# Second norm's squares on ScalarE and adds on VectorE, gate/up operands written between products, last transposes a group later

## Chip, cores and metric

The kernel runs on one core of a Trainium2 chip. The metric is the time of one execution in device microseconds, and the time of a kernel is the median of its runs. In the text PE is TensorE, PEld its weight loads, DVE VectorE, ACT ScalarE, POOL GpSimd and SP SyncE; ACT, DVE, POOL and SP also issue transfers. L1208 is line 1208 of the kernel before; lines of the kernel after are named as such.

## The reference

One decoder layer on x of 512 tokens by 1024 features, all float32. The part around the change is the second half:

```python
mix = jnp.concatenate([y_ml, y_ssd, y_ret], axis=-1)
x = x + mix @ w_out
h = rmsnorm(x, norm_ffn)                      # x * rsqrt(mean(x*x) + 1e-6) * g
gate, up = jnp.split(h @ w_gate_up, 2, axis=-1)
return x + (jax.nn.silu(gate) * up) @ w_down  # then the final rmsnorm
```

Ahead of it stand the first rmsnorm, one wide input projection, and three groups of mixer heads (mLSTM, Mamba-2, retention), which the change does not touch.

## The kernel before

Each float32 matmul is done as three on pairs: an operand is split into `hi` (rounded to float32r) and `lo` (the rest), and a product is hi·hi + hi·lo + lo·hi. Weights come in chunks of 128x1024; `split` (L211, L212) makes a chunk's `hi` by a cast on ACT and its `lo` by a subtraction on DVE. There are four buffers of each, and PE frees one when it has used a chunk, so the splits run some three chunks ahead of PE.

**Output projection.** `products_f` (L427 to L429) multiplies the mixer's result by w_out. `ev_out` evacuates each of eight row blocks x2[k] (L1160, DVE, from PSUM plus the residual), scales it by the norm's weight into y2 (L1164, ACT) and stores x2d (L1165). For odd blocks of the first four it also makes the operands "11" and "S3" with `split_a`: a cast on ACT (L1147) and a subtraction on DVE (L1148).

**Gate and up.** The columns go in blocks p of widths 5x512 and 256. Each block is seven products in the manner of Strassen, "11", "S3", "S1", "S2", "12", "S4", "22" in this order (`product`; L1207 takes `hi` of both, L1208 the weights' `lo`, L1209 the operand's `lo`). Each reads two chunks of weights and one operand of y2, or a sum of blocks of y2 made by `combine` (L1153). Some weight chunks are themselves sums: on `big` buffers they are added by DVE (L952), or by an accumulating load that POOL issues (L194), which waits for the earlier load into the same buffer. `more_loads` issues two such quarters.

**Second norm.** `Norm.feed` squares the x2 blocks in place, the odd ones on POOL (L328), the even ones on ACT (L330), and adds them in a tree on POOL (L334). `finish` sums over the partitions by four matmuls with ones (L340), copies the result (L342, ACT), and takes the power -1/2 on POOL (L306, L286). The result `r2` scales the gate inside the Silu (L1270, ACT), so the products need not wait for it.

**Transposes and down projection.** `turn` makes closures that transpose 128x128 tiles of silu(gate)·up (L1218); `turn_one` runs one between later products. The last of them run in the down projection. That one goes over chunks n and row groups c, each with two banks; for n = 0 the residual is transposed into the banks first (L1314), then L1317 to L1319 multiply. Operands are split by `split_t` (ACT, and POOL at L1296).

**Order.** A scheduler sets the order on each engine from its own estimates, on the basis of the order of the code, except for what is wrapped in `pin`, which keeps its place. An engine runs its instructions in that order; one that waits holds up all behind it.

Of the kernel before, what the change touches and what calls it, by code (L numbers as in the profile page):

```python
# [11 lines left out]
AF = mybir.ActivationFunctionType  # L12
ALU = mybir.AluOpType
# [3 lines left out]
P = 128  # L17
# [102 lines left out]
def trunk(tc, x, xt, wcat, vecs, rows, consts, posn, gfin, out):  # L120
# [6 lines left out]
    with contextlib.ExitStack() as es:  # L127
# [190 lines left out]
        class Norm:  # L318
# [836 lines left out]
        for last in (False, True):  # L1155
            for gr in range(2):

                def ev_out(t, ps):
                    d = x2[4 * gr + t]
                    dve.tensor_tensor(out=d, in0=ps, in1=d, op=ALU.add)  # L1160
                    if last:
# [3 lines left out]
                        sp.dma_start(out=x2d[k], in_=d)  # L1165
                        if t % 2 and gr == 0:
# [13 lines left out]
        s1 = [combine(dve, halves(i, 1), halves(2 + i, 1), ALU.subtract) for i in range(2)]  # L1180
        for i in range(2):
            split_a("S1", i, s1[i])
        s2 = [combine(dve, s1[i], halves(i, 0), ALU.subtract) for i in range(2)]
        for i in range(2):
            split_a("S2", i, s2[i])
        for i in range(2):
            split_a("12", i, halves(2 + i, 0))
        s4 = [combine(pool, halves(2 + i, 0), s2[i], ALU.add) for i in range(2)]
        for i in range(2):
            split_a("22", i, halves(2 + i, 1))  # L1190
        for i in range(2):
            split_a("S4", i, s4[i])
        for k in range(KD):
            n2.feed(x2[k], k % 2 == 1, adds=pool, own=False)
        more_loads()
# [38 lines left out]
        for p, w in enumerate(GU_W):  # L1234
# [4 lines left out]
            for c in range(2):  # L1239
                act.copy(out=s1[c], in_=ba[c][:, 0:w])  # L1240
            bb = [bank() for _ in range(2)]
            product(bb, "S3", w, True)
            e = [slot(w=w) for _ in range(2)]
# [8 lines left out]
            product(bq, "S1", w, True)  # L1252
            turn_one()
            product(bb, "S2", w, False)
            if p == 0:
                n2.finish(r2)
# [10 lines left out]
            product(ba, "12", w, False)  # L1267
            g1 = [slot(w=w) for _ in range(2)]
# [32 lines left out]
        for n, kc in enumerate(DOWN_ORDER):  # L1301
            w2 = [chunk(), chunk()]
            split_t(n + 2)
            for c in range(NC):
                if n == 0 and c == 2:
                    while tail:
                        turn_one()
                    banks += [mbank() for _ in range(4)]
                for hf in range(2):
                    whi, wlo = w2[hf]  # L1310
                    o_ = banks[2 * c + hf]
                    if n == 0:
                        for k in range(4):
                            mm(o_[:, k * P:(k + 1) * P], lhsT=x2[4 * hf + k][:, c * P:(c + 1) * P], rhs=ident, start=k == 0, stop=False, is_transpose=True)  # L1314
                    for k in range(2):
                        ah, al = (t[:, c * P:(c + 1) * P] for t in asp[2 * kc + k])
                        mm(o_, lhsT=ah, rhs=whi[:, k, :], start=False, stop=False)  # L1317
                        mm(o_, lhsT=ah, rhs=wlo[:, k, :], start=False, stop=False)  # L1318
                        mm(o_, lhsT=al, rhs=whi[:, k, :], start=False, stop=n == NK2 - 1 and k == 1)  # L1319
                if n == NK2 - 1:  # L1320
                    ss, rf = small(2, "ssf", bufs=4), small(1, "rf", bufs=4)
                    t = [slot() for _ in range(2)]
                    for hf in range(2):
                        o_ = banks[2 * c + hf]
                        act.activation(out=t[hf], in_=o_, func=AF.Square, accum_out=ss[:, hf:hf + 1])
                    pool.tensor_scalar(out=ss[:, 0:1], in0=ss[:, 0:1], scalar1=1.0 / D, scalar2=EPS, op0=ALU.mult, op1=ALU.add)
                    dve.scalar_tensor_tensor(out=rf, in0=ss[:, 1:2], scalar=1.0 / D, in1=ss[:, 0:1], op0=ALU.mult, op1=ALU.add)
                    rsq(rf)
                    for hf in range(2):
                        y = slot()  # L1330
                        dve.tensor_tensor(out=y, in0=banks[2 * c + hf], in1=gf[hf], op=ALU.mult)
                        if hf == 0:
                            act.activation(out=y, in_=y, func=AF.Copy, scale=rf)
                        else:
                            dve.tensor_scalar(out=y, in0=y, scalar1=rf, scalar2=None, op0=ALU.mult)
                        (act if hf else sp).dma_start(out=out[c, :, 512 * hf:512 * hf + 512], in_=y)
# [70 lines left out]
```

## Time and profile before

| | |
|---|---|
| time, median of 3 runs | 846.32 us (844.91 to 847.32) |
| profiled execution | 845.48 us, span 843.7 us |
| mean granted clock of TensorE | 0.996 |
| busy: PE, PEld | 826.8 us (98%), 710.7 us (84%) |
| busy: DVE, ACT, POOL | 536.7 us (64%), 382.8 us (45%), 256.2 us (30%) |
| transfers | 110.72 MB, mean 131 GB/s |

PE is busy nearly all of the span. What can be gained without taking matmuls away are the places at which it waits, and those at which it runs below its full clock. The wide table of groups counts for little here; the list of waits, the timelines of single engines and the table of stretches tell what stands at such a place.

### The profile page before, as it was taken

What the parts mean: (1) busy time and instruction counts of PE and PEld (TensorE: products, weight loads), DVE (VectorE), ACT (ScalarE), POOL (GpSimd) and SP (SyncE); (2) the same over time, 40 slices, a digit from 0 to 9 for tenths busy, and PEclk for the clock granted to TensorE, in tenths of its full rate; (3) what the DMA queues carried; (4) which work ended last, traced back from release to release, by engine and by line L of the source; (5) the groups of instructions that cost most, each with busy time, mean ns of one, the idle gap of its engine ahead of it and who ended that gap; (6) DMA issues with size and microseconds to landing.
All of it is one profiled execution on the core that took longest, in us unless ns stands there. A gap on an engine that the chain in (4) does not pass through costs nothing.

```text
span 843.7 us, 11298 instructions
## 1 busy us (share of the span) xinstructions
PE 826.8 (98%) x4238; PEld 710.7 (84%) x4238; DVE 536.7 (64%) x760; ACT 382.8 (45%) x655; POOL 256.2 (30%) x261
## 2 busy tenths in 40 slices
PE   9999999999999899999999989999999999999997
PEld 8989889898988788888888868888888889788885
DVE  6648667594739878466633799887878778332223
ACT  6344535464534354335312474646455557511113
POOL 3234524242013966531600573000010103840001
PEclk9999999999999999999999999999999999999999
DMA  7423242332323323224823469686675559330002
GB/s 254 157 65 120 83 142 83 94 113 88 101 83 98 119 76 125 75 75 151 274 101 113 125 191 245 198 252 175 183 190 139 107 147 385 124 100 0 1 1 99
DMA packets 38262, 110.72 MB, mean 131 GB/s; under 512 B 4392, under 2 KB 4776, under 8 KB 38208
## 3 DMA queue, kind: packets, MB, share of 16 engines
q1 hardware_dynamic: 33744, 96.93, 34.2%
q0 software_dynamic: 3456, 11.54, 7.8%
q10 hardware_dynamic: 1008, 1.54, 0.5%
q8 instruction: 33, 0.54, 0.3%
q14 instruction: 21, 0.17, 0.1%
HBM read 104.70 MB, written 5.29 MB: 130 GB/s over the span
## 4 chain that ended last, share of the span: by engine, by line
PE 62%; DVE 5%; POOL 2%; issue 1%; DMA 1%; ACT 1%; POOLq 0%; SPq 0%; ACTq 0%; DVEq 0%
PE b L1207 6%; PE b L1209 6%; PE b L1208 6%; PE b L428 4%; PE b L427 4%; PE b L429 4%; PE b L409 3%; PE b L411 3%; PE b L410 3%; PE m L1208 3%; PE m L1209 2%; PE m L1207 2%; PE m L1319 2%; PE m L1318 2%; PE m L1317 2%; PE b L1317 2%
## 5 line engine op out<-in xcount | busy, mean ns | idle before, releaser
L212 DVE TENSOR_TENSOR lo<-raw,hi 128x1024 fp32r<-128x1024 f32 (+3 forms) x97 | 118.2, 1222 | 116.1 <-ACT hi L211 115.7
L211 ACT CAST hi<-raw 128x1024 fp32r<-128x1024 f32 (+3 forms) x106 | 103.2, 977 | 149.3 <-PE b L428 77.4
L212 DVE TENSOR_TENSOR lo<-big,hi 128x1024 fp32r<-128x1024 f32 (+1 forms) x79 | 97.3, 1234 | 88.3 <-ACT hi L211 86.0
L211 ACT CAST hi<-big 128x1024 fp32r<-128x1024 f32 (+1 forms) x79 | 78.1, 991 | 125.7 <-PE m L1319 57.3
L427 PE MATMUL b<-s,hi 128*128 128x512 f32 x304 | 120.1, 396 | 0.8 <-ACT s L677 0.8
L428 PE MATMUL b<-s,hi 128*128 128x512 f32 x304 | 119.0, 392 | 0.0
L429 PE MATMUL b<-s,lo 128*128 128x512 f32 x304 | 118.5, 391 | 0.0
L410 PE MATMUL b<-lo,s 128*128 128x384 f32 (+2 forms) x320 | 115.2, 360 | 0.8 <-DVE lo L212 0.8
L409 PE MATMUL b<-hi,s 128*128 128x384 f32 (+2 forms) x320 | 114.2, 366 | 0.0
L411 PE MATMUL b<-hi,s 128*128 128x384 f32 (+2 forms) x320 | 113.6, 361 | 0.0
L1208 PE MATMUL b<-lo,s 128*128 128x512 f32 (+1 forms) x240 | 89.7, 374 | 0.0
L1209 PE MATMUL b<-hi,s 128*128 128x512 f32 (+1 forms) x240 | 89.3, 372 | 0.0
L1207 PE MATMUL b<-hi,s 128*128 128x512 f32 (+1 forms) x240 | 88.6, 378 | 0.0
L427 PEld LDWEIGHTS b<-s,hi 128*128 128x128 f32 x304 | 57.1, 188 | 12.1 <-ACT s L677 1.1
L429 PEld LDWEIGHTS b<-s,lo 128*128 128x128 f32 x304 | 57.1, 188 | 11.6
L428 PEld LDWEIGHTS b<-s,hi 128*128 128x128 f32 x304 | 57.2, 188 | 11.0
L410 PEld LDWEIGHTS b<-lo,s 128*128 128x128 f32 x320 | 60.2, 188 | 6.0 <-DVE lo L212 1.2
L409 PEld LDWEIGHTS b<-hi,s 128*128 128x128 f32 x320 | 60.0, 188 | 5.1 <-ACT hi L211 0.3
L411 PEld LDWEIGHTS b<-hi,s 128*128 128x128 f32 x320 | 59.9, 188 | 4.9
L658 DVE SCALAR_TENSOR_TENSOR s<-s,vec,s 128x511 f32<-128x511 f32 (+2 forms) x66 | 58.4, 928 | 0.2 <-ACT s L655 0.2
L194 POOL DMA_DIRECT2D big<-in_wcat x19 | 16.8, 884 | 136.4 <-DMA big<-in_wcat 105.3
L1208 PEld LDWEIGHTS b<-lo,s 128*128 128x128 f32 x240 | 45.3, 189 | 8.0 <-DVE lo L212 0.3
(294 smaller groups left out, 1560.0 us busy)
## 6 DMA issues: line engine op xcount, KB each, us to landing
raw<-in_wcat SPq DMA_DIRECT2D x70, 512.0 KB, 3.4
big<-in_wcat SPq DMA_DIRECT2D x54, 512.0 KB, 4.4
big<-in_wcat POOLq DMA_DIRECT2D x17, 512.0 KB, 7.9
raw<-in_wcat SPq DMA_DIRECT2D x20, 384.0 KB, 3.0
s<-in_xt SPq DMA_DIRECT2D x16, 256.0 KB, 6.7
s<-mdr SPq DMA_DIRECT2D x12, 256.0 KB, 4.3
s<-adr SPq DMA_DIRECT2D x12, 256.0 KB, 5.3
x2d<-s SPq DMA_DIRECT2D x8, 256.0 KB, 2.2
```

The source lines that it names most:

```text
L211: pin(act.copy(out=hi, in_=raw), first)
L212: pin(eng.tensor_tensor(out=lo, in0=raw, in1=hi.bitcast(F32), op=ALU.subtract), first)
L409: mm(o_, lhsT=hh, rhs=whi[:, k, :], start=kk == 0, stop=False)
L410: mm(o_, lhsT=hh, rhs=wlo[:, k, :], start=False, stop=False)
L411: mm(o_, lhsT=hl, rhs=whi[:, k, :], start=False, stop=kk == KD - 1)
L427: mm(banks[t], lhsT=wh, rhs=rhs_hi[kk], start=a, stop=False)
L428: mm(banks[t], lhsT=wh, rhs=rhs_lo[kk], start=False, stop=False)
L429: mm(banks[t], lhsT=wl, rhs=rhs_hi[kk], start=False, stop=b)
L658: dve.scalar_tensor_tensor(out=a[:, sft:S], in0=u[:, 0:S - sft], scalar=w[3 - sft], in1=a[:, sft:S], op0=ALU.mult, op1=ALU.add)
L1207: mm(o_, lhsT=ah, rhs=whi[:, k, :], start=first and s_ == 0 and k == 0, stop=False, skip_group_check=not first)
L1208: mm(o_, lhsT=ah, rhs=wlo[:, k, :], start=False, stop=False, skip_group_check=not first)
L1209: mm(o_, lhsT=al, rhs=whi[:, k, :], start=False, stop=s_ == 1 and k == 1, skip_group_check=not first)
```

## The change

It has three parts.

1. *Second norm.* The squares of the first four x2 blocks are taken in `ev_out`, into buffers of their own; those of the last four stand behind the third product, in place. All eight are on ACT, and the seven adds are on DVE. `finish` is called behind the product "12", no longer behind "S2".
2. *Operands.* The S2 operands are made behind the first product, those of "12", "22" and "S4", and `more_loads`, behind the second.
3. *Down projection.* The order of groups is (0,0), (0,1), (0,2), (1,0), (0,3), and then as before; the remaining transposes run behind (0,2), where they stood ahead of it; two of the banks are taken at a time.

```diff
-            def feed(self, x_, on_pool, adds=dve, own=True):
+            def feed(self, x_, on_pool, own=True):
                 k, sq = len(self.sq), self.sq
                 sq.append(slot() if own else x_)
                 if on_pool:
-                    pool.tensor_tensor(out=sq[k], in0=x_, in1=x_, op=ALU.mult)
+                    pin(pool.tensor_tensor(out=sq[k], in0=x_, in1=x_, op=ALU.mult), not own)
                 else:
-                    pin(act.activation(out=sq[k], in_=x_, func=AF.Square), self is n1)
+                    pin(act.activation(out=sq[k], in_=x_, func=AF.Square), self is n1 or not own)
...
-                    adds.tensor_tensor(out=sq[i], in0=sq[i], in1=sq[j], op=ALU.add)
+                    dve.tensor_tensor(out=sq[i], in0=sq[i], in1=sq[j], op=ALU.add)
...
                         sp.dma_start(out=x2d[k], in_=d)
+                        if gr == 0:
+                            n2.feed(d, False)
...
-        s2 = [combine(dve, s1[i], halves(i, 0), ALU.subtract) for i in range(2)]
...
-        for k in range(KD):
-            n2.feed(x2[k], k % 2 == 1, adds=pool, own=False)
-        more_loads()
+        def after_first():
+            s2 = [combine(dve, s1_[i], halves(i, 0), ALU.subtract) for i in range(2)]
+            for i in range(2):
+                split_a("S2", i, s2[i])
+            return s2
+
+        def after_second(s2):
+            for i in range(2):
+                split_a("12", i, halves(2 + i, 0))
+            s4 = [combine(pool, halves(2 + i, 0), s2[i], ALU.add) for i in range(2)]
+            for i in range(2):
+                split_a("22", i, halves(2 + i, 1))
+            for i in range(2):
+                split_a("S4", i, s4[i])
+            more_loads()
+
+        def after_third():
+            for k in range(4, KD):
+                n2.feed(x2[k], False, own=False)
...
             product(bb, "S2", w, False)
-            if p == 0:
-                n2.finish(r2)
...
             product(ba, "12", w, False)
+            if p == 0:
+                n2.finish(r2)
...
+        order = [(n, c) for n in range(NK2) for c in range(NC)]
+        order[3:5] = [(1, 0), (0, 3)]
...
+            while (n, c) == (0, 2) and tail:
+                turn_one()
```

What this moves on the engines is told by their orders. A name such as s_4491 is a buffer with its number; numbers differ between the kernels.

POOL, from the norm's last adds to the loads behind r2. Before (s_3844 to s_3858 are the squares, big_... in L194 the weight buffers, r_840_4476 is r2):

```order
L334 TENSOR_TENSOR s_3852<-s_3852,s_3856 128x512
L334 TENSOR_TENSOR s_3844<-s_3844,s_3852 128x512
L1153 TENSOR_TENSOR s_4509<-big_4294,s_4489 128x512
L1153 TENSOR_TENSOR s_4511<-big_4295,s_4491 128x512
L194 DMA big_4296<-in_wcat 128x1024 x2
L306 TENSOR_SCALAR r_840_4476<-ss_4707 128x4
L286 TENSOR_TENSOR r_840_4476<-r_840_4476,mhalf_111 128x4
L194 DMA big_4295<-in_wcat 128x1024 x2
```

After, in the same place:

```order
L1153 TENSOR_TENSOR s_4375<-big_4294 128x512
L1153 TENSOR_TENSOR s_4409<-big_4294 128x512
L1153 TENSOR_TENSOR s_4598<-big_4294,s_4542 128x512
L1153 TENSOR_TENSOR s_4600<-big_4295,s_4544 128x512
L194 DMA big_4296<-in_wcat 128x1024 x2
L194 DMA big_4295<-in_wcat 128x1024 x2
L306 TENSOR_SCALAR r_844_4487<-ss_4755 128x4
L286 TENSOR_TENSOR r_844_4487<-r_844_4487,mhalf_111 128x4
```

The squares and adds are gone from POOL, four L1153 are left, and the second pair of accumulating loads now stands ahead of the two instructions that make r2.

DVE, at the operands of "S1" and "S2" (s_4477 and s_4479 before, s_4488 and s_4490 after, are the two S1 sums; lo_4571 and lo_4523 are the `lo` of the first chunk of "S1"). Before:

```order
L212 TENSOR_TENSOR lo_4551<-raw_4299,hi_4550 128x1024
L1153 TENSOR_TENSOR s_4479<-big_4294,big_4295 128x512
L1148 TENSOR_TENSOR s_4482<-s_4477,s_4481 128x512
L1148 TENSOR_TENSOR s_4486<-s_4479,s_4485 128x512
L1153 TENSOR_TENSOR s_4489<-s_4477,big_4294 128x512
L1153 TENSOR_TENSOR s_4491<-s_4479,big_4294 128x512
L212 TENSOR_TENSOR lo_4571<-big_4296,hi_4570 128x1024
```

After:

```order
L212 TENSOR_TENSOR lo_4503<-raw_4299,hi_4502 128x1024
L1153 TENSOR_TENSOR s_4490<-big_4294,big_4295 128x512
L1148 TENSOR_TENSOR s_4493<-s_4488,s_4492 128x512
L1148 TENSOR_TENSOR s_4497<-s_4490,s_4496 128x512
L1153 TENSOR_TENSOR s_4542<-s_4488,big_4294 128x512
L1153 TENSOR_TENSOR s_4544<-s_4490,big_4294 128x512
L212 TENSOR_TENSOR lo_4523<-big_4296,hi_4522 128x1024
```

The order here is the same in both: the two S2 combinations stand ahead of the split in the scheduled order, though the code now makes them later. Three L334 adds have come in between the evacuations ahead of these rows, four behind them.

PE, at the end of "S1" (bank m) and what follows (hi_4592 before and hi_4556 after are its second chunk, hi_4650 before and hi_4646 after the first of "12", hi_4610 the first of "S2"). Before:

```order
L1208 MATMUL m_4631<-lo_4593,s_4485 128x512
L1209 MATMUL m_4631<-hi_4592,s_4486 128x512
L340 MATMUL m_4702<-ones_105,s_3844 128x1 x4
L1207 MATMUL b_4548<-hi_4650,s_4501 128x512
L1207 MATMUL b_4549<-hi_4650,s_4501 128x512
L1207 MATMUL b_4590<-hi_4610,s_4493 128x512
L1208 MATMUL b_4590<-lo_4611,s_4493 128x512
```

After:

```order
L1217 MATMUL m_4627<-hi_4556,s_4496 128x512
L1218 MATMUL m_4627<-lo_4557,s_4496 128x512
L1219 MATMUL m_4627<-hi_4556,s_4497 128x512
L1217 MATMUL b_4500<-hi_4646,s_4590 128x512
L1217 MATMUL b_4501<-hi_4646,s_4590 128x512
L1218 MATMUL b_4500<-lo_4647,s_4590 128x512
L1219 MATMUL b_4500<-hi_4646,s_4591 128x512
```

The norm's matmuls (L340) have left this place for one behind both chunks of "12". Of the first chunk of "12" only the two matmuls that need `hi` alone stood ahead of "S2"; now the whole chunk does, with those that need `lo`.

PE, at the start of the down projection: the last transposes (L1218 before, L1228 after; s_6245 and s_6246 before, s_6249 and s_6250 after, are what L1280 makes last). Before:

```order
L1319 MATMUL b_6399<-hi_6348,s_6405 128x512
L1218 MATMUL m_6474<-kst_72,s_6245 128x128
L1218 MATMUL m_6481<-kst_72,s_6142 128x128
L1218 MATMUL m_6474<-kst_72,s_6246 128x128
L1218 MATMUL m_6481<-kst_72,s_6245 128x128
L1218 MATMUL m_6481<-kst_72,s_6246 128x128
L1318 MATMUL m_6488<-lo_6328,s_6400 128x512
```

After:

```order
L1339 MATMUL b_6403<-hi_6352,s_6409 128x512
L1339 MATMUL m_6478<-hi_6331,s_6409 128x512
L1338 MATMUL m_6479<-lo_6353,s_6404 128x512
L1339 MATMUL m_6479<-hi_6352,s_6405 128x512
L1337 MATMUL m_6479<-hi_6352,s_6408 128x512
L1338 MATMUL m_6479<-lo_6353,s_6408 128x512
L1339 MATMUL m_6479<-hi_6352,s_6409 128x512
L1228 MATMUL m_6500<-kst_72,s_6249 128x128
L1228 MATMUL m_6500<-kst_72,s_6250 128x128
```

b_6399 and b_6403 are the last bank of group (0,1), m_6488 and m_6478 the first of group (0,2). The transposes of what L1280 makes have moved behind group (0,2).

## Rows read from the trace of the kernel before

**Rows 1.** PE's waits from 400 to 520: engine, line, awaited: total us, times, longest us.

```profile
PE m L1208 <- DVE lo L212: 3.2, 1, 3.2
```

**Rows 2.** PE's timeline around "S1": start us, us, instruction, count, [idle before].

```profile
495.62 0.61 PE L1207 MATMUL m<-hi,s 128*128 128x512 f32 x2
499.39 0.80 PE L1208 MATMUL m<-lo,s 128*128 128x512 f32 x1 [3.16 <-DVE lo L212]
...
502.87 0.40 PE L1208 MATMUL m<-lo,s 128*128 128x512 f32 x1
503.10 0.40 PE L1209 MATMUL m<-hi,s 128*128 128x512 f32 x1
```

**Rows 3.** Stretches: us; busy us (count) of PE, PEld, DVE, ACT, POOL; PEclk, DMA, GB/s.

```profile
496.00:499.40 3.40, 0.24 (x3) 0.01 (x1) 3.40 (x3) 2.33 (x5) 3.32 (x3) 0.99 0.69 196
499.40:503.00 3.60, 3.60 (x9) 2.88 (x10) 3.60 (x2) 3.14 (x6) 3.30 (x2) 0.54 0.75 261
503.00:515.00 12.00, 12.00 (x59) 9.98 (x58) 11.93 (x15) 6.47 (x10) 7.06 (x4) 1.00 0.93 235
```

**Rows 4.** Groups of DVE, 472 to 500: count | busy us, mean ns | idle.

```profile
L212 DVE TENSOR_TENSOR lo<-big,hi 128x1024 fp32r<-128x1024 f32 x3 | 6.6, 2216 | 0.0
L1148 DVE TENSOR_TENSOR s<-s,s 128x512 fp32r<-128x512 f32 x4 | 5.1, 1280 | 0.6 <-ACT s L1147 0.5
L1160 DVE TENSOR_TENSOR s<-b,s 128x512 f32<-128x512 f32 x7 | 4.7, 679 | 0.0
L1153 DVE TENSOR_TENSOR s<-s,big 128x512 f32<-128x512 f32 x2 | 3.5, 1776 | 0.0
```

**Rows 5.** DVE's timeline, 487 to 509.

```profile
487.80 0.68 DVE L1160 TENSOR_TENSOR s<-b,s 128x512 f32<-128x512 f32 x1
...
505.51 1.88 DVE L1148 TENSOR_TENSOR s<-big,s 128x512 fp32r<-128x512 f32 x3
507.32 1.21 DVE L212 TENSOR_TENSOR lo<-big,hi 128x1024 fp32r<-128x1024 f32 x1
```

**Rows 6.** Groups of POOL, 472 to 500.

```profile
L334 POOL TENSOR_TENSOR s<-s,s 128x512 f32<-128x512 f32 x7 | 12.6, 1805 | 0.4
L328 POOL TENSOR_TENSOR s<-s 128x512 f32<-128x512 f32 x4 | 5.4, 1344 | 3.5 <-DMA x2d<-s 1.6 <-ACT s L330 1.1 <-ACT s L1147 0.8
```

**Rows 7.** ACT's timeline: a square, a cast, the Silus and their table.

```profile
473.10 0.62 ACT L330 ACTIVATE s<-s 128x512 f32<-128x512 f32 x1
...
503.53 1.05 ACT L211 CAST hi<-big 128x1024 fp32r<-128x1024 f32 x1 [0.18 <-PE m L1209]
...
516.80 1.28 ACT L1270 ACT_TABLE_LOAD   x1 [0.31 <-PE b L1209]
518.10 1.27 ACT L1270 ACTIVATE s<-b,r 128x512 f32<-128x512 f32 x2
```

**Rows 8.** POOL's timeline: first norm, then from 498 to 520.

```profile
23.88 0.45 POOL L306 TENSOR_SCALAR r<-ss 128x4 f32<-128x4 f32 x1 [5.32 <-ACT ss L342]
...
498.22 4.48 POOL L1153 TENSOR_TENSOR s<-big,s 128x512 f32<-128x512 f32 x2
...
507.63 3.30 POOL L306 TENSOR_SCALAR r<-ss 128x4 f32<-128x4 f32 x1 [0.21 <-ACT ss L342]
511.01 2.02 POOL L286 TENSOR_TENSOR r<-r,mhalf 128x4 f32<-128x4 f32 x1
...
519.35 0.86 POOL L194 DMA_DIRECT2D big<-in_wcat  x1 [0.54 <-DMA big<-in_wcat]
```

**Rows 9.** PE's timeline at the first matmul of column block 1.

```profile
529.14 0.71 PE L1207 MATMUL b<-hi,s 128*128 128x512 f32 x2
```

**Rows 10.** PE's and DVE's timelines at the last transposes.

```profile
720.13 0.44 PE L1218 MATMUL m<-kst,s 128*128 128x128 f32 x2 [0.31 <-DVE s L1280]
721.53 0.55 PE L1218 MATMUL m<-kst,s 128*128 128x128 f32 x3 [0.97 <-DVE s L1280]
...
718.56 2.92 DVE L1280 SCALAR_TENSOR_TENSOR s<-s,r,s 128x256 f32<-128x256 f32 x2
```

More of the change, by code (lines that the diff above doesn't have):

```diff
@@ L1179, in trunk @@
         r2 = small(NC, "r2")
-        s1 = [combine(dve, halves(i, 1), halves(2 + i, 1), ALU.subtract) for i in range(2)]
+        s1_ = [combine(dve, halves(i, 1), halves(2 + i, 1), ALU.subtract) for i in range(2)]
         for i in range(2):
-            split_a("S1", i, s1[i])
-        s2 = [combine(dve, s1[i], halves(i, 0), ALU.subtract) for i in range(2)]
[L1184 to L1192, printed above, removed]
-        for k in range(KD):
-            n2.feed(x2[k], k % 2 == 1, adds=pool, own=False)
-        more_loads()
+            split_a("S1", i, s1_[i])
+        def after_first():
[15 more added lines that the diff above has]
+                n2.feed(x2[k], False, own=False)
         aT = [None] * (2 * len(DOWN_ORDER))
@@ L1240, in trunk @@
                 act.copy(out=s1[c], in_=ba[c][:, 0:w])
+            s2 = after_first() if p == 0 else None
             bb = [bank() for _ in range(2)]
             product(bb, "S3", w, True)
+            if p == 0:
+                after_second(s2)
             e = [slot(w=w) for _ in range(2)]
@@ L1300, in trunk @@
         split_t(1)
[L1301 to L1308, printed above, removed]
+        order = [(n, c) for n in range(NK2) for c in range(NC)]
+        order[3:5] = [(1, 0), (0, 3)]
+        w2s = {}
+        for n, c in order:
+            kc = DOWN_ORDER[n]
+            if n not in w2s:
+                w2s[n] = [chunk(), chunk()]
+                split_t(n + 2)
+            w2 = w2s[n]
+            if n == 0 and c >= 2:
+                banks += [mbank() for _ in range(2)]
+            for hf in range(2):
+                whi, wlo = w2[hf]
+                o_ = banks[2 * c + hf]
+                if n == 0:
+                    for k in range(4):
+                        mm(o_[:, k * P:(k + 1) * P], lhsT=x2[4 * hf + k][:, c * P:(c + 1) * P], rhs=ident, start=k == 0, stop=False, is_transpose=True)
+                for k in range(2):
+                    ah, al = (t[:, c * P:(c + 1) * P] for t in asp[2 * kc + k])
+                    mm(o_, lhsT=ah, rhs=whi[:, k, :], start=False, stop=False)
+                    mm(o_, lhsT=ah, rhs=wlo[:, k, :], start=False, stop=False)
+                    mm(o_, lhsT=al, rhs=whi[:, k, :], start=False, stop=n == NK2 - 1 and k == 1)
+            while (n, c) == (0, 2) and tail:
+                turn_one()
+            if n == NK2 - 1:
+                ss, rf = small(2, "ssf", bufs=4), small(1, "rf", bufs=4)
+                t = [slot() for _ in range(2)]
@@ L1309, in trunk @@
                 for hf in range(2):
-                    whi, wlo = w2[hf]
                     o_ = banks[2 * c + hf]
[L1312 to L1336, printed above, removed]
+                    act.activation(out=t[hf], in_=o_, func=AF.Square, accum_out=ss[:, hf:hf + 1])
@@ new lines, in trunk @@
+                pool.tensor_scalar(out=ss[:, 0:1], in0=ss[:, 0:1], scalar1=1.0 / D, scalar2=EPS, op0=ALU.mult, op1=ALU.add)
+                dve.scalar_tensor_tensor(out=rf, in0=ss[:, 1:2], scalar=1.0 / D, in1=ss[:, 0:1], op0=ALU.mult, op1=ALU.add)
+                rsq(rf)
+                for hf in range(2):
+                    y = slot()
+                    dve.tensor_tensor(out=y, in0=banks[2 * c + hf], in1=gf[hf], op=ALU.mult)
+                    if hf == 0:
+                        act.activation(out=y, in_=y, func=AF.Copy, scale=rf)
+                    else:
+                        dve.tensor_scalar(out=y, in0=y, scalar1=rf, scalar2=None, op0=ALU.mult)
+                    (act if hf else sp).dma_start(out=out[c, :, 512 * hf:512 * hf + 512], in_=y)
```

3 lines of the change are left out of this document (added).

## Prediction

> **What bounds the kernel now.** I read the list of PE's waits first. Inside the stretch that the change touches it has one of 3.2 us, of an L1208 matmul for the DVE `lo` split at L212 [rows 1]; a second place, at the last transposes, is far smaller [rows 10]. PE's timeline places the first: the two first matmuls of product "S1" need only `hi` and start at 495.62, the next one needs `lo` and starts at 499.39, after 3.16 us of idling [rows 2]. The table of stretches says what is full there: in 496.00 to 499.40 PE works 0.24 us, DVE 3.40 of 3.40, POOL 3.32. In 499.40 to 503.00, after that idle time, PE runs at a granted clock of 0.54, near its lower level of 1.2 GHz, and from 503.00 on at 1.00, the level of 2.4 GHz [rows 3]. So the bound there is DVE's queue, and PE pays twice: for the wait, and for a slow restart.
>
> Why is DVE late? From 472 to 500 its operations with two SBUF inputs took 1.28 to 2.22 us on average, while the evacuations at L1160, with one input in PSUM, took 0.68 [rows 4]. From 505.51 three L1148 took 1.88 together, 0.63 each, and an L212 1.21 [rows 5], with the DMA share at 0.93 [rows 3]. So the transfers are not the cause. What had ended by then was POOL's last L1153, at 502.70 [rows 8]; what ran beside the slow ones were seven L334 adds of 12.6 us and four L328 squares of 5.4 us [rows 6]. Against 0.63 and 1.21 the groups of rows 4 lose 2.6 us (four L1148), 2.2 us (two L1153) and 2.0 us (the two L212 that end before 499.4): 6.8 us.
>
> **The change part by part.**
>
> *Norm moved off POOL.* POOL loses the seven adds and four squares, 18.0 us [rows 6]. ACT gets four more squares of 0.62 us [rows 7]. DVE gets seven adds; by the order of DVE three of them stand ahead of the awaited split, 3 x 0.63 = 1.9 us. Otherwise DVE's order around that split is the same: the two S2 combinations still stand ahead of it, though the code makes them later. What changes is how long each operation takes. From the last evacuation at 487.80 [rows 5] to the end of the awaited split at 499.34, 11.5 us, stand L1160, L212, L1153, two L1148, two L1153 and that L212. Undisturbed they are 0.60 + 1.21 + 0.63 + 1.26 + 1.26 + 1.21 = 6.2 us, and with half a microsecond for ACT's casts in between 6.7: ready at 494.5 even with no earlier start. The L1153 that stay on POOL can slow two of them by 1.1 us each, as the L1153 of 1.78 against 0.63: 496.7 at worst. Of the 6.8 us lost some 3.0 lie ahead of 487.80 (all but the two L1153, one L212 and half a microsecond of L1148); less the 1.9 us of adds, the queue can start 1.1 us earlier: 493.4 at best. I take 494.5 and PE arrives at 496.07, so the wait goes: **-3.16 us**. At the worst end 0.6 us of it stays.
> With it goes the slow restart: from 499.39 to 502.87 are eight steps of matmuls, 3.48 us, which at the 0.23 us of the next step [rows 2] are 1.82: **-1.66 us**. Its bounds are 0 and -1.66; I take all of it, since the trace shows the lower level only behind the idle time.
>
> *What is late next.* PE's new order runs the first chunk of "12" (hi_4646, lo_4647) right behind "S1". There are four `hi` buffers, so hi_4646 waits until PE lets go of S1's first chunk, at 496.07 + 12 x 0.23 = 498.8; a cast of 1.05 [rows 7] and a split of 1.21 give 501.1, with two hand-overs of 0.2 (the 0.18 ahead of the cast in rows 7) 501.5. PE gets there at 498.8 + 2.7 = 501.5. On DVE nine operations (seven L1148, two L212: 6.8 us) stand between the two splits: 494.5 + 6.8 + 1.2 = 502.5. So the new wait is 0 to 1.4 us, the high end with POOL's last L1153 beside it; I take **+0.8**. ACT's four squares stand ahead of the copies that free the bank of "S2", 4 x 0.62 = 2.5 us; "12" running first covers that with its 2.7 us. I put it at nothing, and at 1 to 2 us if that cover fails.
>
> *r2.* The norm's matmuls now follow "12": 501.5 + 0.8 + 2.7 + 5.4 + 2.7 = 513.1. But POOL has two L194 loads ahead of L306 and L286 that it had behind them. The second was issued at 519.35, for 0.86 us, waiting for an earlier load to land; L306 took 3.30 us and L286 2.02, and the first norm's L306 0.45 [rows 8]. If the loads move along with PE by 4 us, this one is issued at 515.4, done at 516.2, and r2 is there at 518.8 to 521.6. Who waits: the Silus (table load 1.28, two of them 1.27), behind them on ACT's queue the first cast of column block 1 (1.05) [rows 7], on DVE its split (1.21): 4.8 us, 5.6 with four hand-overs. PE's first matmul of that block starts at 529.14 [rows 9]; moved by 4 us, 525.1, and its third, the first to need `lo`, 0.45 later. So r2 costs nothing up to about 519.9, and up to 1.7 us at 521.6. I take **+0.3**, as the middle, 520.2, is 0.3 behind the limit.
> Here a rule speaks against the change. The row first: L306, of 128x4 elements, took 3.30 us while DVE worked without a pause, and 0.45 at 23.88 [rows 8]. The Trainium skill (page "SBUF — State Buffer", section "Who interferes with whom") says that a DVE operation with two SBUF inputs contends with GpSimd's reads for a shared pair of ports, and that whoever issues first holds it for the whole instruction while the other fully blocks. By that rule the adds given to DVE hold up L306 again, r2 comes at the late end, and the sum is -3.6 instead of -5.0; the row agrees.
>
> *Last transposes.* Before, the transposes of the last products stand behind group (0,1) and wait 0.31 and 0.97 us for two L1280 that start at 718.56 and take 2.92 [rows 10]. Now eleven matmuls and four residual transposes more stand ahead of them, at least 11 x 0.23 = 2.5 us, more than the two waits: **-1.28 us**, unless DVE is later there by over 1.2 us.
>
> *The rest.* There are as many matmuls as before, and the operands of "12", "22" and "S4" are made at nearly the same place of each queue. I put this at 0.
>
> **Sum**: -3.16 - 1.66 + 0.8 + 0.3 - 1.28 = -5.0 us. Against the profiled execution's 845.48 that is 840.5; the median of the runs is 0.84 higher, which I add: 841.3. With nothing new late it is 840.2; the lowest run of before lay 1.4 us under its median, which gives 838.8 as low end. With the bad ends of two of the terms it is 843.5.
>
> **Rivals.**
> 1. *The gain is partly given back by the weights.* PE runs 4 to 5 us earlier into a stretch where the DMA share is 0.93 over 12 us [rows 3], which leaves 0.8 us. If the loads can't move along, PE or r2 waits for them, and 1 to 3 us come back: 842 to 844.5. For it: the 0.93. Against it: PE's list has no wait there but the one [rows 1], and most of those loads wait for buffers that PE frees.
> 2. *DVE stays slow.* The L1153 that stay on POOL, 2.24 us each at 498.22 [rows 8], or something else do the same harm. Then the split stays late, the three adds cost 0 to 1.9 us more, and only the tail's 1.28 us is gained: 845.0 to 847. Against it: eleven of POOL's operations go, and rows 5 show DVE undisturbed without them.
> 3. *r2 becomes the bound, and the kernel slower.* If the second load is still issued at 519.35, r2 comes at 519.35 + 0.86 + 0.1 + 3.30 + 2.02 = 525.6, 5.7 us behind the limit, and PE restarts at the lower clock (1.7 us): -5.3 + 5.7 + 1.7 = +2.1 us, 848.4, and a microsecond more for each by which the load is later. It eats the whole gain from an issue at about 517.2 on, and is slower by over 0.3% from about 519.8. For it: loads on POOL's queue that wait for other loads. Against it: what those wait for are buffers that PE frees earlier now.
> 4. *The change does not do what it says*, because the order comes from a scheduler. The orders show the adds and the transposes moved, and the S2 operands not; the sum counts only what moved, so this has no price of its own.
>
> **How the numbers follow.** A measurement of this kernel can tell about 0.3%, 2.5 us, from no change: the bounds are 843.8 and 848.9. The chances are 0.62 for the forecast (838.8 to 843.5), 0.19 for rival 1, 0.11 for rival 2, 0.06 for rival 3 and 0.02 for less than 838.8. Faster: 0.62 + 0.02 + 0.12 of rival 1 = 0.76. Same: the rest of rival 1 (0.07), rival 2 and 0.02 of rival 3 = 0.20. Slower: 0.04. The range from 838.8 to 845.5 takes in the forecast, rival 1 and the low end of rival 2, about 0.84.
>
> **What would show it.** Right: no wait of an "S1" matmul on L212 and a granted clock of 1.00 from 496 to 503; L1148 and L1153 on DVE at 0.6 to 0.7 us; a wait of up to 1.4 us at the first chunk of "12"; r2 before 521; no wait for the last products' transposes. Wrong: DVE operations still at 1.1 to 1.8 us with the adds gone from POOL (rival 2); waits of PE for loads between 500 and 520 (rival 1); block 1's first matmuls waiting for a split that stands behind the Silus (rival 3).

## The result, and the profile after

The median of five runs of the kernel after is 840.51 us (839.7 to 842.46) against 846.32 us before: a ratio of 0.9937, 95% interval 0.9918 to 0.9957. The profiled execution took 839.70 us with a span of 837.9, 5.8 us less than before; forecast were 5.0.

PE's list of waits from 400 to 520 has one row again, but it is another one (lines are those of the kernel after, in which L1217 to L1219 are the matmuls of `product`):

```profile
PE b L1218 <- DVE lo L212: 1.2, 1, 1.2
```

PE's timeline, at the start of "S1" and at the start of "12", answers [rows 2]. The columns are start us, us, instruction, count, and the idle time before it:

```profile
495.44 0.62 PE L1217 MATMUL m<-hi,s 128*128 128x512 f32 x2
495.89 0.39 PE L1218 MATMUL m<-lo,s 128*128 128x512 f32 x1
...
500.88 0.61 PE L1217 MATMUL b<-hi,s 128*128 128x512 f32 x2
502.69 0.50 PE L1218 MATMUL b<-lo,s 128*128 128x512 f32 x1 [1.20 <-DVE lo L212]
```

"S1" starts its third matmul 0.45 us behind its first, with no idle time, where it had idled 3.16 us. The first chunk of "12" now waits 1.20 us for its `lo`. The table of stretches, with the cuts of [rows 3], shows the second half of the gain:

```profile
496.00:499.40 3.40, 3.40 (x17) 2.81 (x16) 3.40 (x6) 2.77 (x5) 1.53 (x2) 1.00 0.85 186
499.40:503.00 3.60, 2.40 (x11) 1.70 (x10) 3.60 (x5) 3.60 (x9) 0.21 (x1) 1.00 1.01 216
```

In the two stretches in which PE had worked 0.24 us and then run at 0.54, it now runs at 1.00, with 1.20 us of idling in the second. POOL is nearly out of them, 1.53 and 0.21 us. DVE's groups from 472 to 500 answer [rows 4]:

```profile
L212 DVE TENSOR_TENSOR lo<-big,hi 128x1024 fp32r<-128x1024 f32 x5 | 8.2, 1655 | 0.0
L1160 DVE TENSOR_TENSOR s<-b,s 128x512 f32<-128x512 f32 x7 | 4.8, 680 | 0.0
L1148 DVE TENSOR_TENSOR s<-s,s 128x512 fp32r<-128x512 f32 x6 | 4.5, 766 | 0.1
...
L1153 DVE TENSOR_TENSOR s<-s,big 128x512 f32<-128x512 f32 x2 | 1.3, 684 | 0.0
```

L1153 fell from 1776 to 684 ns, L1148 from 1280 to 766, while the evacuations at L1160 stayed at 680. Some of the five L212 are still slow: two at 490.46, the splits of "S1", take 4.56 us, beside the two L1153 that POOL runs from 490.11 to 493.94. DVE's timeline and POOL's:

```profile
490.46 4.56 DVE L212 TENSOR_TENSOR lo<-big,hi 128x1024 fp32r<-128x1024 f32 x2
490.11 3.83 POOL L1153 TENSOR_TENSOR s<-big,s 128x512 f32<-128x512 f32 x2 [11.51 <-ACT hi L211]
```

To see which part of PE's time went where, count its matmuls: all kernels here run 4238. The 2600th starts in the first product of gate and up, ahead of every matmul that the change puts in another place; the 3600th in the last column block; the 3800th in the down projection, behind the transposes. The table gives how much later (+) or earlier (-) each profiled execution is at those places than the kernel before, in us, worked out from PE's timelines, and what each stretch adds.

| kernel | at 2600 | 2600 to 3600 | 3600 to 3800 | to the last | ratio to before (95%) |
|---|---|---|---|---|---|
| after | -0.18 | -3.86 | -1.77 | 0.00 | 0.9937 (0.9918 to 0.9957) |
| e2 tail only | +0.92 | 0.00 | -1.77 | 0.00 | 0.9974 (0.9962 to 0.9987) |
| e3 norm only | +1.30 | -3.60 | 0.00 | 0.00 | 0.9954 (0.9942 to 0.9966) |
| e4 operands only | +1.64 | +0.24 | -0.01 | 0.00 | 1.0008 (0.9999 to 1.0016) |
| e5 after and dead adds | +0.52 | +6.61 | -1.77 | 0.00 | 1.0059 (1.0045 to 1.0072) |
| e6 splits later | -0.05 | -0.83 | -1.77 | 0.00 | 0.9973 (0.9961 to 0.9985) |
| e7 norm and tail | +0.41 | -4.17 | -1.77 | 0.00 | 0.9925 (0.9912 to 0.9938) |
| e8 r2 late, 12 | -0.38 | -3.68 | -1.77 | 0.00 | 0.9923 (0.9910 to 0.9935) |
| e9 r2 late, 30 | -0.20 | +3.26 | -1.77 | 0.00 | 0.9988 (0.9977 to 0.9999) |
| e10 splits and loads | +2.18 | +2.97 | -1.77 | 0.00 | 0.9992 (0.9981 to 1.0003) |
| e11 S4 and loads | +0.49 | -2.10 | -1.76 | 0.00 | 0.9964 (0.9951 to 0.9976) |
| e12 after again | -0.27 | -3.89 | -1.76 | 0.00 | 0.9927 (0.9913 to 0.9940) |
| e13 norm and tail again | +1.62 | -4.27 | -1.77 | 0.00 | 0.9927 (0.9915 to 0.9940) |

The first column is not the change: but for e5 it is the same already at the 2400th matmul, in the output projection, where the executions differ by up to 2.8 us. A single profiled span is therefore a poor measure of an edit that is worth 2 us, and the columns behind it a better one. In e5 alone something is added in between (-0.59 at the 2400th, +0.52 at the 2600th), most of it a wait of 0.61 us at 487.83 for an evacuation on DVE.

The tail's timeline answers [rows 10]:

```profile
718.21 0.39 PE L1339 MATMUL m<-hi,s 128*128 128x512 f32 x1
718.44 0.82 PE L1228 MATMUL m<-kst,s 128*128 128x128 f32 x6
```

Six transposes run in one piece, with no idle time ahead of them.

### The profile page after: what moved, and what is told of

Same layout as the page of the kernel before. It is cut to its first block, busy times and chain, and to the rows that moved or that the text cites. A ratio compares the mean times of both kernels' runs of the same rounds, so it can differ in the third digit from the quotient of the medians.

```text
span 837.9 us, 11283 instructions
## 1 busy us (share of the span) xinstructions
PE 825.2 (98%) x4238; PEld 711.0 (85%) x4238; DVE 531.6 (63%) x767; ACT 384.3 (46%) x659; POOL 235.1 (28%) x250
## 4 chain that ended last, share of the span: by engine, by line
PE 62%; DVE 6%; POOL 1%; issue 1%; ACT 1%; DMA 0%; POOLq 0%; SPq 0%
PE b L1218 6%; PE b L1219 6%; PE b L1217 6%; PE b L428 4%; PE b L427 4%; PE b L429 4%; PE b L409 3%; PE b L411 3%; PE b L410 3%; PE b L1337 2%; PE b L1338 2%; PE b L1339 2%; PE m L1337 2%; PE m L1338 2%; PE m L1339 2%; PE m L1217 2%
## 5 line engine op out<-in xcount | busy, mean ns | idle before, releaser
L212 DVE TENSOR_TENSOR lo<-raw,hi 128x1024 fp32r<-128x1024 f32 (+3 forms) x97 | 117.2, 1212 | 116.5 <-ACT hi L211 116.0
L212 DVE TENSOR_TENSOR lo<-big,hi 128x1024 fp32r<-128x1024 f32 (+1 forms) x79 | 96.9, 1230 | 87.7 <-ACT hi L211 86.3
L1218 PE MATMUL b<-lo,s 128*128 128x512 f32 (+1 forms) x240 | 89.7, 374 | 1.2 <-DVE lo L212 1.2
L1219 PE MATMUL b<-hi,s 128*128 128x512 f32 (+1 forms) x240 | 89.3, 372 | 0.0
L1217 PE MATMUL b<-hi,s 128*128 128x512 f32 (+1 forms) x240 | 88.4, 378 | 0.0
L194 POOL DMA_DIRECT2D big<-in_wcat x19 | 16.8, 882 | 145.1 <-DMA big<-in_wcat 116.9
L1218 PEld LDWEIGHTS b<-lo,s 128*128 128x128 f32 x240 | 45.2, 189 | 9.4 <-DVE lo L212 1.6
```

What stands on the lines that cost most here:

```text
L212: pin(eng.tensor_tensor(out=lo, in0=raw, in1=hi.bitcast(F32), op=ALU.subtract), first)
L1217: mm(o_, lhsT=ah, rhs=whi[:, k, :], start=first and s_ == 0 and k == 0, stop=False, skip_group_check=not first)
L1218: mm(o_, lhsT=ah, rhs=wlo[:, k, :], start=False, stop=False, skip_group_check=not first)
L1219: mm(o_, lhsT=al, rhs=whi[:, k, :], start=False, stop=s_ == 1 and k == 1, skip_group_check=not first)
```

## The experiments

Two theories stood against each other. **P**: POOL's squares and adds slowed DVE's operations with two SBUF inputs; taking them off POOL is what removed the wait. **O**: the place in the code at which the operands are made did it.

**e5: the contention put back alone.** The kernel after, with eleven additions on POOL that nobody reads, one or two as each block is evacuated. PE and ACT keep their order, and DVE's differs by two neighbours.

```diff
                         if gr == 0:
                             n2.feed(d, False)
+                        for _ in range((0, 1, 1, 1, 2, 2, 2, 2)[k]):
+                            pool.tensor_tensor(out=junk, in0=x2[k - 1], in1=d, op=ALU.add)
```

> The kernel after with eleven additions on POOL that nobody reads (128x512, two SBUF inputs, each of two x2 blocks as they are evacuated), as many as the norm's operations that went from POOL; the orders of PE and ACT are those of after, DVE's has two neighbours swapped. Theory P: L1148, L1153 and L212 on DVE from 472 to 500 are back at 1.1 to 2.3 us, the first S1 matmul that needs lo waits 3 to 5 us and the granted clock falls behind it: span 842.5 to 846.0 against 837.9. Rival O: DVE undisturbed, no wait at S1, 837.2 to 838.6.

Measured: span 849.0, ratio 1.0059. The two longest waits of PE between 400 and 530 (two more are of 0.6 and 0.4 us), then DVE's groups from 472 to 500 (L1161 is the evacuation in this kernel), then the stretches:

```profile
PE m L1221 <- DVE lo L212: 5.1, 1, 5.1
PE b L1221 <- DVE lo L212: 2.7, 1, 2.7
```

```profile
L1148 DVE TENSOR_TENSOR s<-s,s 128x512 fp32r<-128x512 f32 x4 | 5.9, 1500 | 0.0
L1161 DVE TENSOR_TENSOR s<-b,s 128x512 f32<-128x512 f32 x6 | 4.1, 679 | 0.0
...
L1153 DVE TENSOR_TENSOR s<-s,big 128x512 f32<-128x512 f32 x2 | 2.3, 1212 | 0.0
```

```profile
496.00:502.40 6.40, 1.03 (x4) 0.30 (x2) 6.40 (x6) 4.82 (x8) 5.60 (x4) 0.71 0.28 80
502.40:506.00 3.60, 3.51 (x9) 2.86 (x10) 3.60 (x5) 2.96 (x5) 1.17 (x1) 0.56 0.91 327
506.00:512.20 6.20, 3.65 (x16) 2.65 (x15) 6.20 (x9) 5.56 (x9) 1.74 (x2) 1.00 0.87 194
512.20:515.90 3.70, 3.57 (x9) 2.85 (x10) 3.70 (x6) 0.00 (x0) 0.00 (x0) 0.54 0.97 237
```

DVE's L1148 are back at 1500 ns and its L1153 at 1212, while the evacuations stay at 679. DVE doesn't idle (0.0 in these rows, 6.40 of 6.40 us in the first stretch), so it is late by the length of its operations and not by waiting for a result of POOL. PE waits 5.1 us at "S1" and then runs at 0.56, waits 2.7 us at "12" and runs at 0.54. This shows P for POOL's work as a whole. The eleven are all additions and take POOL 20.8 us, where the norm had seven adds and four squares of 18.0 us, so the share of the squares is not shown. It cost more than I expected, since the damage is paid a second time at "12": that product's split stands in the same queue. The Trainium skill (page "SBUF — State Buffer", section "Who interferes with whom") says that a DVE instruction with at most one SBUF input, outside its 2-port performance modes, does not contend with GpSimd, and that one with two SBUF inputs contends with a GpSimd instruction that reads SBUF. By that, the split into 679 and 1500 ns is what is to be seen; the trace agrees.

**e4: the second part alone.** The kernel before, with the S2 operands made behind "11" and the rest, the norm included, behind "S3".

```diff
-        s2 = [combine(dve, s1[i], halves(i, 0), ALU.subtract) for i in range(2)]
...
+        def after_first():
+            s2 = [combine(dve, s1_[i], halves(i, 0), ALU.subtract) for i in range(2)]
...
+        def after_second(s2):
...
+            for k in range(KD):
+                n2.feed(x2[k], k % 2 == 1, adds=pool, own=False)
+            more_loads()
```

> The kernel before with the second part alone (operands made between the products; norm on POOL, tail as before). The scheduler answers by putting the first S1 split on DVE ahead of the two S2 combinations, and the second behind them. Theory P: the operations beside POOL still take 1.1 to 2.3 us; the wait for the first split falls to 0 to 0.9 us, the second split is late by 0.5 to 2.5 us instead: span 840.5 to 843.0. Rival O (order is enough): no wait at S1, no low clock, 838.2 to 839.2.

Measured: ratio 1.0008 (0.9999 to 1.0016), no gain: +0.24 us in the stretch. The scheduler did put the first S1 split ahead of the two combinations, and DVE's timeline shows it ready in time but the next one late:

```profile
495.25 2.31 DVE L212 TENSOR_TENSOR lo<-big,hi 128x1024 fp32r<-128x1024 f32 x1
497.49 3.48 DVE L1153 TENSOR_TENSOR s<-s,big 128x512 f32<-128x512 f32 x2
500.89 1.21 DVE L212 TENSOR_TENSOR lo<-big,hi 128x1024 fp32r<-128x1024 f32 x1
```

The combinations at 497.49 take 3.48 us beside POOL's adds, and the second split ends at 502.1. PE's waits are two then, and the stretches show the second of them followed by the lower clock:

```profile
PE m L1214 <- DVE lo L212: 1.5, 1, 1.5
PE b L1213 <- ACT hi L211: 1.4, 1, 1.4
```

```profile
502.00:506.00 4.00, 3.57 (x19) 3.03 (x19) 4.00 (x4) 4.00 (x7) 2.75 (x3) 1.00 0.87 209
506.00:508.00 2.00, 0.88 (x2) 0.50 (x2) 2.00 (x3) 2.00 (x5) 0.00 (x0) 0.77 1.02 264
508.00:510.40 2.40, 2.40 (x6) 1.82 (x6) 2.40 (x4) 1.65 (x4) 0.00 (x0) 0.50 0.59 188
```

O is refuted, and P's number was too good as well: I expected 0.7 to 3.2 us less than before. The late DVE queue held up ACT's cast for "12" too (ACT waits 2.23 and 1.08 us for the two combinations, and the casts stand behind), and I hadn't counted a second wait with a restart at 0.50.

**e3: the first part alone.** The kernel before with the norm's squares on ACT, adds on DVE, and `finish` behind "12".

```diff
+                        if gr == 0:
+                            n2.feed(d, False)
...
-        for k in range(KD):
-            n2.feed(x2[k], k % 2 == 1, adds=pool, own=False)
         more_loads()
...
             product(bq, "S1", w, True)
+            if p == 0:
+                for k in range(4, KD):
+                    n2.feed(x2[k], False, own=False)
...
             product(ba, "12", w, False)
+            if p == 0:
+                n2.finish(r2)
```

> The kernel before with the first part alone (squares on ACT, adds on DVE, finish behind product 12; operands made where they were, tail as before). DVE's order around the awaited split is that of before, and S2 stays ahead of 12 on PE. Theory P (POOL's adds and squares slowed DVE): L1153 and L1148 on DVE fall to 0.6 to 0.7 us, the wait at S1 goes with the low clock, nothing waits at 12, the tail's two waits stay: span 838.2 to 839.4, about 5.0 us less than before and some 0.5 to 1.5 more than after. Rival O (it was the order in which the operands are made): the 3.2 us wait stays and three adds come on top, 843.7 to 845.6.

Measured: span 841.4, of which 1.30 us lie ahead of the change; in the stretch -3.60. The wait at "S1" and the low clock are gone and nothing waits at "12", as P has it. But 0.90 us came in that I had not expected: the norm's matmuls wait for the last add. The waits of PE, then the timelines of POOL, ACT and PE at r2 and behind it:

```profile
PE m L340 <- DVE s L334: 0.9, 1, 0.9
...
520.95 0.86 POOL L194 DMA_DIRECT2D big<-in_wcat  x1 [7.54 <-DMA big<-in_wcat]
521.88 0.20 POOL L306 TENSOR_SCALAR r<-ss 128x4 f32<-128x4 f32 x1
...
523.23 1.27 ACT L1273 ACTIVATE s<-b,r 128x512 f32<-128x512 f32 x2 [5.95 <-POOL r L286]
...
529.99 0.50 PE L1207 MATMUL b<-hi,s 128*128 128x512 f32 x1 [0.21 <-ACT hi L211]
```

The last row is a second loss: r2 comes at 523.19, the Silus hold up ACT's casts of block 1, and PE waits for one of them.

So the first part alone makes nearly all of the gain of the middle stretch (-3.60 of -3.86), and it makes it with the operands where they were.

**e2: the third part alone.**

```diff
-        for n, kc in enumerate(DOWN_ORDER):
...
+        order = [(n, c) for n in range(NK2) for c in range(NC)]
+        order[3:5] = [(1, 0), (0, 3)]
...
+            while (n, c) == (0, 2) and tail:
+                turn_one()
```

> The kernel before with the third part alone (order of the groups of the down projection, last transposes behind group (0,2)). Both theories: the two waits of the transposes for L1280 (0.31 and 0.97 us) go, the 3.2 us wait at S1 and the stretch at the lower clock stay. Span 842.0 to 842.6 against 843.7, that is 1.1 to 1.7 us less. If what the transposes waited for is merely met by another wait there, the span stays at 843.7.

Measured: exactly -1.77 us between the 3600th and the 3800th matmul, the same as in every kernel with this part; both waits are gone from the list. The span of 842.8 has 0.92 us from ahead of the change in it.

**e7, e12, e13: is the second part worth anything beside the other two?** e7 and e13 are one kernel, e3's edit and e2's together; e12 is the kernel after once more, run beside e13.

```diff
+ the edits of e3_norm_only and e2_tail_only, without after_first and after_second
```

> The kernel before with the first and the third part (norm and tail), without the second. The parts add up: the norm alone gained 3.5 us behind the output projection, the tail alone 1.7 us of PE's time: 5.2 us together, so 838.5 where the stretch ahead of the change runs as in the profile before. If the second part is worth anything, the kernel after is faster than this one by over 0.5 us; if not, they are the same within 0.4 us.

> The kernel after once more, on the same chip and in the same call as the next, to compare the two: 0.9937 of before, 840 to 841. If the second part is worth nothing beside the other two, the medians of this and of norm and tail without it lie within 0.7 us of each other.

> The kernel before with the norm and tail parts, without the second, once more beside the kernel after. Its profile had no wait at 12 (1.20 us in after) but one of 0.90 us of the norm's matmuls for the last add: the same time as after within 0.7 us, 839.5 to 841.

Measured: e7 839.84 us; then, on one chip, after 839.85 (839.54 to 840.53) and without the second part 839.77 (839.38 to 841.05). The parts add up: -4.17 and -4.27 in the stretch and -1.77 in the tail. The stretch gains 0.6 us more than in e3, though the orders of PE, ACT and DVE are the same there; that is the loss at block 1, which came in e3 alone. The second part is worth nothing that the medians show, and by the stretch it costs 0.3 to 0.4 us (-3.86 and -3.89 with it). It trades one wait for another: with it 1.20 us at "12", without it 0.90 us at the norm's matmuls.

**e6, e10, e11: can the wait at "12" be taken away?** In the kernel after, ACT's timeline and DVE's show what that split waited for:

```profile
498.36 1.05 ACT L211 CAST hi<-big 128x1024 fp32r<-128x1024 f32 x1 [0.62 <-PE m L1219]
...
499.09 1.21 DVE L212 TENSOR_TENSOR lo<-big,hi 128x1024 fp32r<-128x1024 f32 x1
500.22 0.68 DVE L1148 TENSOR_TENSOR s<-big,s 128x512 fp32r<-128x512 f32 x1
500.82 0.68 DVE L1148 TENSOR_TENSOR s<-s,s 128x512 fp32r<-128x512 f32 x1
501.43 1.21 DVE L212 TENSOR_TENSOR lo<-big,hi 128x1024 fp32r<-128x1024 f32 x1
```

The buffer of `hi` is free in time: the cast at 498.36 waited 0.62 us for PE and ended at 499.41. DVE comes to the split at 501.43 without having idled; two L1148 of operands that are needed later and an L212 stand ahead of it. So I moved those operands behind the third product: in e6 without `more_loads`, in e10 with it, in e11 those of "S4" alone.

```diff
         def after_second(s2):
             for i in range(2):
                 split_a("12", i, halves(2 + i, 0))
             s4 = [combine(pool, halves(2 + i, 0), s2[i], ALU.add) for i in range(2)]
-            for i in range(2):
-                split_a("22", i, halves(2 + i, 1))
-            for i in range(2):
-                split_a("S4", i, s4[i])
             more_loads()
+            return s4
...
-        def after_third():
+        def after_third(s4):
             for k in range(4, KD):
                 n2.feed(x2[k], False, own=False)
+            for i in range(2):
+                split_a("22", i, halves(2 + i, 1))
+            for i in range(2):
+                split_a("S4", i, s4[i])
```

These three have as many matmuls and compute another result. In e6 the operands of "22" are read from y2 after later weights have been loaded over it. In e10 and e11, by the order of the code, the first chunk of "12" is split ahead of the load that `more_loads` issues for it.

> The kernel after, with the squares of the last four blocks and then the operands of 22 and S4 made behind the third product (the operands of 12, the S4 sums and more_loads stay behind the second). On DVE only two L1148 instead of five now stand between the two splits of S1 and the first split of 12, and PE runs S2 ahead of 12. If DVE's queue made the wait at 12 in the kernel after (1.20 us idle), it goes and nothing takes its place: 1.2 to 1.4 us less than after from the output projection to the end, span about 836.5. If it was the buffer of hi (freed by S1's first chunk), the first split is late all the same, at S2 or at 12: 837.9 as after.

> The kernel after with, behind the third product: the last four squares, the operands of 22 and S4, and more_loads, in this order, so that no load overwrites y2 ahead of its last reader. PE runs S2 ahead of 12, and the first split of 12 has until some 506.8 instead of 501.3. If DVE's queue made the 1.20 us wait at 12, it goes: 1.2 to 1.4 us less than after behind the output projection, span near 836.5. Against it: the loads now start up to 5 us later into a stretch with a DMA share of 0.9; if those bind, the sums at L952 and the splits of S4 and 22 are late by 1 to 3 us, span 838 to 840.

> The same, but the operands of 22 stay behind the second product; behind the third stand S4's operands, the squares and more_loads. S2 again ahead of 12 on PE. The same numbers: 836.5 if only DVE's queue bound, 838 to 840 if the later loads do.

Measured: the wait at "12" is gone in all three, and e6 and e11 reach the norm's matmuls earlier than after (1.2 and 1.5 us, corrected for the first column). But PE waits behind them in its place: 1.76 us for L212 in e6, 1.59 us for L212 in e10, 0.61 us for a cast and 0.45 us for an evacuation in e11. In e10 it waits again at block 1, 2.23 and 0.64 us, and then runs at 0.53. Less is left of the gain in the stretch than in after (-0.83, +2.97, -2.10 against -3.86), and the 1.2 to 1.4 us forecast for each did not come. In e10 and e11 the casts stand idle for 4.0 and 4.6 us until a sum at L952 is made, at 512.63 and 511.56 against 508.38 in after; in e10 the landing of a load releases it, in e11 it follows in DVE's queue without idle time. In e6 two of ACT's casts wait 2.0 us each for the loads over y2. None beats after, and none computes the layer. That DVE's queue is the limit at "12" is read from the rows above; a clean removal wasn't found.

**e8 and e9: how late may r2 be?** The kernel after with 12 or 30 multiplications by one of the 128x4 sums on POOL, ahead of L306.

```diff
                 act.copy(out=ss, in_=ps[:, 0:NC])
+                for _ in range(12 if self is not n1 else 0):
+                    pool.tensor_scalar(out=ss, in0=ss, scalar1=1.0, scalar2=0.0, op0=ALU.mult, op1=ALU.add)
```

> The kernel after with twelve multiplications by one of the 128x4 sums on POOL ahead of L306: r2 comes some 3.4 us later, near 522.9 instead of 519.47, all else alike. By the prediction's limit for r2 (519.9) PE waits 3.0 us at the first matmuls of column block 1: span 840.9. By the trace of after (the lo split of block 1's first chunk is ready at 522.97 and wanted at 525.55, so the limit is near 522.0) it waits 0.5 to 1.2 us: span 838.4 to 839.1. If r2 doesn't matter at all: 837.9.

> The same with thirty such multiplications: r2 some 8.4 us later, near 527.9. By the trace of after PE waits 5.9 us and then restarts at the lower clock (1.7 us): span 845 to 846. By the prediction's limit 8.0 us and 1.7: 847.6. If r2 doesn't matter: 837.9.

e8, POOL's timeline and ACT's:

```profile
517.58 5.23 POOL L344 TENSOR_SCALAR ss<-ss 128x4 f32<-128x4 f32 x12
...
523.16 1.03 POOL L286 TENSOR_TENSOR r<-r,mhalf 128x4 f32<-128x4 f32 x1
...
516.97 1.05 ACT L211 CAST hi<-big 128x1024 fp32r<-128x1024 f32 x1 [2.52 <-PE b L1221]
...
524.23 1.27 ACT L1287 ACTIVATE s<-b,r 128x512 f32<-128x512 f32 x2 [4.92 <-POOL r L286]
```

r2 came 4.7 us later, at 524.19, and neither of the two waits forecast came: -3.68 in the stretch against -3.86, and a ratio of 0.9923. The scheduler, which counts the twelve instructions, had put block 1's first cast (516.97) ahead of the Silus (524.23), so nothing on PE's path stood behind r2 any more. The run thus says that r2 need not bind, and leaves open where the limit lies in the order of after; of that e3 and e7 tell more (below, at r2). In e9 r2 comes at 530.25 and PE waits:

```profile
PE b L1219 <- ACT s L1287: 4.2, 1, 4.2
```

Here the bank that a Silu still reads is what PE wants, and with the lower clock behind it (0.50 from 530 to 534) the stretch takes 7.1 us more than in after. The expected span of 845 to 846 was met by 845.0, but not by its working: the wait is 4.2 us and not 5.9, and for a bank, not for a split. A late r2 can thus bind, as rival 3 has it; in this order of ACT that begins near 526.0 (530.25 less 4.2, an estimate), 6.5 us behind the r2 of after.

## Why the prediction was right, point by point

- **The wait at "S1"** (-3.16): right, and for the reason given, as e5 and e3 show. I put the split at 494.5 (493.4 to 496.7); it was ready at 492.78, outside that range and 3.1 us ahead of its use. The queue started earlier than I allowed: the last evacuation began at 485.55, 2.25 us earlier than before, where I reckoned with 1.1 at best. I had summed the lost time of three groups of rows 4, and others ahead of it were slowed too: two L1148 that read `big` took 1228 ns on average before and 679 after, an L212 on `raw` 1.71 us and then 1.21. From that evacuation on DVE was no faster than I thought, 7.2 us against 6.7, since the split itself took 2.32 us beside an L1153 on POOL. In PE's steps the wait was worth 3.32 us: the two matmuls from 495.62 are due a third at 496.07, and it came at 499.39.
- **The slow restart** (-1.66): right. The granted clock is 1.00 through the stretch.
- **The new wait at "12"** (+0.8, 0 to 1.4): right in place and cause, and nearly in size, 1.20 us idle. Of the two limits that I worked out, the buffer (501.5) and DVE's queue (502.5), the queue decided: the split ended at 502.64. That this is so near was luck in part. The queue was 1.7 us ahead at the first split, but ten operations stood between the two and not nine (three L212, the first of 2.31 us beside POOL's last L1153), 9.9 us instead of 8.0.
- **r2** (+0.3): no cost, and the working was wrong in three places. These are the rows, on POOL, ACT and DVE:

```profile
517.23 0.86 POOL L194 DMA_DIRECT2D big<-in_wcat  x1 [6.51 <-DMA big<-in_wcat]
518.16 0.19 POOL L306 TENSOR_SCALAR r<-ss 128x4 f32<-128x4 f32 x1
518.44 1.03 POOL L286 TENSOR_TENSOR r<-r,mhalf 128x4 f32<-128x4 f32 x1
...
519.50 1.27 ACT L1285 ACTIVATE s<-b,r 128x512 f32<-128x512 f32 x2 [3.59 <-POOL r L286]
520.66 1.05 ACT L211 CAST hi<-big 128x1024 fp32r<-128x1024 f32 x1
...
521.74 1.23 DVE L212 TENSOR_TENSOR lo<-big,hi 128x1024 fp32r<-128x1024 f32 x1 [4.54 <-ACT hi L211]
```

r2 is there at 519.47, inside the forecast's 518.8 to 521.6, but by two errors that offset each other. The second load was issued at 517.23, only 2.1 us earlier than before and not 4, since it waits for a landing that moved less than PE did. L306 and L286 took 0.19 and 1.03 us, not 3.30 and 2.02: DVE idled 4.54 us until 521.74. In e6, where DVE was at work, L306 took 1.13 us from 517.35, beside an L212 that ended at 518.43. The rule of the Trainium skill (page "SBUF — State Buffer", section "Who interferes with whom"), weighed as the harder case (-3.6), had nothing to act on here, because DVE had no work at that moment.

The third error is the limit of 519.9. I counted ACT's table load (1.28 us) behind r2, but it runs at 514.63, while ACT waits. From r2 to the end of block 1's first split are 3.50 us (519.47 to 522.97) and not 5.6, and the second matmul of that block, the first to need `lo`, is due at 525.33: the limit is near 521.8. e3 and e7, in which the Silus stand ahead of block 1's first cast as here, bear that out. In e7 r2 comes 3.59 us ahead of block 1's first matmul (521.71 and 525.30) and costs next to nothing; in e3 it comes 3.02 us ahead (523.19 and 526.21), and PE loses some 0.6 us on e7 by the 2767th matmul. In after it comes 5.63 us ahead (519.47 and 525.10).

- **Last transposes** (-1.28): right, but under-sized: -1.77. The list of waits counts idle time only from the modelled end of the matmul before, 0.39 us behind its start, where the next one could start 0.23 behind it; that is 0.16 us for each wait, 0.32 of the 0.49 us. I put the rest down to the two broken-up groups of transposes, which was not tested.
- **The rest** (0): right that the second part gains nothing, as e12 and e13 show; wrong that this could be read from the orders being alike. Alone, it makes the scheduler choose another order (e4).
- **The sum**: -3.86 and -1.77 are measured against -3.72 and -1.28, and -0.18 lies ahead of the change: -5.81 at the last matmul. The median, forecast at 841.3, is 840.5.

Of the rivals, 2 is refuted by DVE's groups and by the wait that went; in small it is there, since the two splits of "S1" still take 2.3 us each beside POOL's L1153. Rival 1 did not come: PE has no wait for loads. Its sign is seen in the second L194, which moved by half of PE's gain, and in e10, where a sum at L952 is released by a load. Rival 3 did not come in after, and its mechanism is seen in e3 and e9.

## What to carry to other kernels

A wait for a DVE result can have its cause on POOL: look at which DVE operations are slow (two SBUF inputs) and which are not (one in PSUM), and at what POOL runs beside them, before taking work off DVE itself. Here DVE got seven operations more and was done sooner. Where a scheduler sets the order, an edit made alone can get another order than within the change, as in e4; take it out of the whole as well, and compare at fixed points of the bounding engine, counted in its instructions.

## What was not expected of the hardware

Whether TensorE's clock falls behind a wait isn't told by the wait's length alone. It stayed at 1.00 behind 1.20 us (after), 1.52 us (the first of e4) and 1.59 us (e10), and fell behind 1.76 us (e6, 0.52 from 518 to 520), behind 0.61 and 0.45 us close together in e11, and behind the 1.39 us that are the second wait of e4. PE's timeline and the stretch of e11, and the stretches of e10 for comparison:

```profile
513.99 0.73 PE L1218 MATMUL b<-hi,s 128*128 128x512 f32 x2 [0.61 <-ACT hi L211]
515.17 0.73 PE L1218 MATMUL m<-hi,s 128*128 128x512 f32 x1 [0.45 <-DVE s L1275]
```

```profile
514.00:518.70 4.70, 4.25 (x11) 3.04 (x12) 3.98 (x5) 3.47 (x5) 3.03 (x4) 0.64 0.90 258
```

```profile
515.40:517.30 1.90, 0.40 (x2) 0.00 (x0) 1.90 (x4) 1.88 (x3) 0.86 (x1) 1.00 0.85 224
517.30:523.00 5.70, 5.61 (x25) 4.64 (x26) 3.59 (x5) 2.34 (x4) 2.15 (x3) 1.00 1.02 293
```

In e11 the stretch from 514.0 to 518.7, with 0.45 us of idle time in it, ran at 0.64; in e10 the 1.9 us from 515.4 held 1.5 us of idle time, and both it and the stretch behind it ran at 1.00. What decides whether the clock falls is open.
